# Two-layer diffusion transformer: value products of two heads side by side, scores in three passes, and bias rows and stores moved to other places

## The chip, the cores and the metric

The kernel runs on one core of one Trainium2 chip. The metric is the device time of one execution in microseconds (us), the median of several runs. The engines are TensorE (PE in the profile, its weight loads PEld), VectorE (DVE), ScalarE (ACT), GpSimd (POOL) and SyncE (SP), whose queue starts most transfers.

## The reference

Two layers work on 256 latent and 256 context tokens of width 1024. Each layer mixes tokens along three branches, gates and sums them, projects the sum, and then does a retrieval over 16384 experts by product keys. In the last layer, only the latent tokens have queries, gates and retrieval.

```
for l in range(2):
    m = silu(c) @ ada_w[l] + ada_b[l]            # 6 x 1024 modulation values, for latent and for context
    h = rmsnorm(x) * (1 + scale) + shift         # the same for ctx
    f, p, q, k, v, gates = split(h @ w_in[l])
    # 8 heads of 64, 2 key/value heads; latent queries see 512 keys, context queries 256
    ya = softmax(q @ k.T * 64 ** -0.5) @ v
    yf = fourier(f); yp = pool(p)
    x = x + m[2] * ((g0 * yf + g1 * yp + g2 * ya) @ w_out[l])
    h2 = modulate(rmsnorm(x), m[3], m[4])
    s = einsum(h2 @ wq, keys)                    # 8 heads, two halves, 128 keys each
    ...                                          # top 16 of each half, top 16 of the 256 sums
    x = x + m[5] * sum(softmax(top) * gelu(u[idx] . h2) * v[idx])
```

## The kernel before

Everything is f32 outside and runs in the order in which it is written: each engine works through its instructions in program order, and waits in front of one hold up all behind it on that engine. The helper `load` puts a transfer on SP's queue, which is in order too.

PE's large products go through `mm3`: both operands are split into a high and a low fp32r half (`split_to`: ACT writes the high half, DVE or POOL the low one), and three fp32r passes are summed. Where operands are not split, one f32 matmul stands, which the trace shows as two records: the scores (L667), the transposes of the probabilities (L685), the value products (L700), the modulation products (L333).

Weights come as items of 1 MB through a stream `S` with three raw buffers. `S.take` hands out a loaded item, `S.split` and `S.presplit` also split it, and the load of a later item waits until its buffer has been read.

**Modulation.** `ada_item(l, g, k)` adds the eighth k of group g (2048 of the 6144 values) into one PSUM bank, in four column quarters of 32 rows. At k = 0 it takes a tile `adab` for the biases, zeroes it on POOL and loads four rows with `load`. At k = 7, `finish` adds the biases on DVE. Group 0 goes into columns; groups 1 and 2 are stored to a scratch tensor `md` on SP's queue. The groups of layer 1 are computed inside layer 0: group 0 among the gate products after attention, groups 1 and 2 in the loop over heads h of the retrieval's query projection (`ada_now`).

**Attention.** Keys and queries are normalized and rotated on DVE (`rot`), transposed on PE and copied by ACT into `kT` and `qT`. Items are (pair of heads hc, block of 128 queries b, head of the pair e): 32 in layer 0, 16 in layer 1. A loop handles the scores of item n, the normalization of n - 1, the transposes of n - 2 and the value products of n - 3; steps of a gate product (`filler`, two `mm3` chains each) stand between. 24 such steps belong to the loop and 8 to the time ahead of the transposes. Both heads of a pair write into one bank `ya`, at rows 0 to 63 and 64 to 127.

**Seam after the output projection.** `wout(n, b)` makes a quarter n of the columns for block b, `wout_end(b)` stores a row block of X (`xm`) and starts its norm. `keys()` transposes the retrieval's keys, `nrm.trans(0, q)` and `nrm.cols(0, q)` the normalized latent tiles. The retrieval then projects queries for eight heads h (weights `wq`), DVE takes the top 16 of the key scores (`SC`) of each head, and the u tables follow in steps `st`, with `u_T` transposing on DVE.

Of the kernel before, what the change touches and what calls it, by code (L numbers as in the profile page):

```python
# [60 lines left out]
def kernel(ctx_: ExitStack, tc: tile.TileContext, I, C, out):  # L61
# [256 lines left out]
    md = {}  # L318
    ada_ps, ada_bt = {}, {}

    def ada_item(l, g, k):
        w = S.take(("ada", l, g, k))
        if k == 0:
            ada_ps[l, g] = psum(name="adaps")
            bt = b4([128, 2, 512], name="adab")
            ada_bt[l, g] = bt
            nc.gpsimd.memset(bt[:, 0], 0.0)
            for j in range(4):
                load(out=bt[32 * j:32 * j + 2, 0, :],
                     in_=dram(I["ada_b"], l * 6 * D + g * 2048 + j * 512, [[0, 2], [1, 512]]))  # L330
# [7 lines left out]
        def finish():  # L338
            bt = ada_bt.pop((l, g))
            nc.vector.tensor_tensor(out=bt[:, 1, :], in0=ps, in1=bt[:, 0, :], op=OP.add)  # L340
            if g == 0:
                mix_cols(l, bt[:, 1])
                return
            md[l, g] = dr_p.tile([2, 2048], F32, name=f"md{l}{g}")
            for j in range(4):
                nc.sync.dma_start(out=md[l, g][:, j * 512:(j + 1) * 512], in_=bt[32 * j:32 * j + 2, 1, :])
            if g == 2 and l == 0:
                ffn_rows(l)
# [131 lines left out]
    def mixer(l, nrm, last):  # L480
# [81 lines left out]
        kT = b4([128, 512], name="kT")  # L562
        qT = b8([128, 4, nt], name="qT")
# [79 lines left out]
        for _ in range(8):  # L643
# [4 lines left out]
        nc.scalar.activation(kT, ps, AF.Copy)  # L648
        for j in range(4):
# [3 lines left out]
            nc.scalar.activation(qT[:, j, :], ps[:, :nt], AF.Copy)  # L653
# [5 lines left out]
        def stage_scores(n):  # L659
# [7 lines left out]
            nc.tensor.matmul(ps[:, :nk], lhsT=qT[s, j, b * 128:(b + 1) * 128], rhs=kT[s, kb[0] * 128:kb[1] * 128],  # L667
                             start=True, stop=True)
# [23 lines left out]
        def stage_pv(n):  # L692
            hc, b, e = items[n]
            v = (2 * hc + e) // 4
            pT, kb = st.pop(n)
            if b == 0 and e == 0:
                ya[hc] = psum(name="ya")
            for q in range(kb[0], kb[1]):
                o = (q - kb[0]) * 128
                nc.tensor.matmul(ya[hc][64 * e:64 * e + 64, b * 128:(b + 1) * 128],  # L700
                                 lhsT=KV[:, q, 128 + 64 * v:192 + 64 * v], rhs=pT[:, o:o + 128],
                                 start=q == kb[0], stop=q == kb[1] - 1)
            if b == nq - 1 and e == 1:
# [6 lines left out]
        for n in range(N + 3):  # L710
            if 0 <= n - 1 < N:
                stage_norm(n - 1)
            if n < N:
                stage_scores(n)
# [5 lines left out]
            if n >= 3:  # L720
# [47 lines left out]
    def peer(l, nrm, kT, nb, fin):  # L768
# [263 lines left out]
        for h in range(9):  # L1032
            cur = None
            if h < 8:
                if l + 1 < DEPTH:
# [76 lines left out]
        for st in range(NSTEP):  # L1112
# [29 lines left out]
            if st == NSTEP - 10:  # L1142
                SP["keep"].discard("single")
                SP["free"] = [f for f in SP["free"] if f[1] in SP["keep"]]
                for _ in sd:
                    pass
# [223 lines left out]
```

## Time and profile before

| | us |
|---|---|
| median of 3 runs (2942.41 to 2950.72) | 2943.49 |
| profiled execution | 2943.76 |
| its span in the trace | 2942.0 |
| PE busy (94% of the span) | 2753.4 |
| DVE busy (73%) | 2158.2 |
| ACT busy (47%) | 1375.9 |
| POOL busy (44%) | 1282.2 |

The span is the time from the first to the last instruction of the profiled execution; 1.8 us lie around it. Busy time is what the engine's instructions took. PE's clock has two levels, 1.2 and 2.4 GHz; the granted clock of a stretch is the mean share of the upper one, 0.97 over the span.

### The profile page before, as it was taken

What the parts mean: (1) busy time and instruction counts of PE and PEld (TensorE: products, weight loads), DVE (VectorE), ACT (ScalarE), POOL (GpSimd) and SP (SyncE); (2) the same over time, 40 slices, a digit from 0 to 9 for tenths busy, and PEclk for the clock granted to TensorE, in tenths of its full rate; (3) what the DMA queues carried; (4) which work ended last, traced back from release to release, by engine and by line L of the source; (5) the groups of instructions that cost most, each with busy time, mean ns of one, the idle gap of its engine ahead of it and who ended that gap; (6) DMA issues with size and microseconds to landing.
All of it is one profiled execution on the core that took longest, in us unless ns stands there. A gap on an engine that the chain in (4) does not pass through costs nothing. (4 is left out here: it accounts for less than half of the span.)

```text
span 2942.0 us, 42776 instructions
## 1 busy us (share of the span) xinstructions
PE 2753.4 (94%) x16484; PEld 2403.8 (82%) x16484; DVE 2158.2 (73%) x3388; ACT 1375.9 (47%) x2243; POOL 1282.2 (44%) x698
## 2 busy tenths in 40 slices
PE   6999998799899999999999997998989989899999
PEld 4767786689888889988888886788989989888887
DVE  3444344899999985589999996555988778566666
ACT  3343223134489983333333334545446766544443
POOL 0110003237777778676666662102677655500000
PEclk8999998899999999999999999999999999899999
DMA  6215756558999999999999994337788898967775
GB/s 232 87 44 177 253 186 187 157 120 210 258 286 296 291 297 286 268 361 377 379 376 380 369 362 173 119 123 189 157 194 191 223 223 208 249 250 299 280 296 198
DMA packets 365580, 706.99 MB, mean 240 GB/s; under 512 B 25424, under 2 KB 265456, under 8 KB 351296
## 3 DMA queue, kind: packets, MB, share of 16 engines
q1 hardware_dynamic: 271104, 491.38, 56.0%
q0 software_dynamic: 36864, 134.23, 12.5%
q10 hardware_dynamic: 57408, 78.65, 7.9%
q8 instruction: 129, 2.11, 0.3%
q14 instruction: 75, 0.61, 0.1%
HBM read 619.18 MB, written 85.00 MB: 239 GB/s over the span
## 5 line engine op out<-in xcount | busy, mean ns | idle before, releaser
L1180 PE MATMUL acc<-hl,A 128*128 128x512 f32 x3840 | 871.2, 389 | 0.0
L1180 PEld LDWEIGHTS acc<-hl,A 128*128 128x128 f32 x3840 | 720.6, 188 | 150.1 <-ACT A L287 0.5
L1025 POOL TENSOR_TENSOR hl<-UT,hl 128x1024 fp32r<-128x1024 f32 x256 | 629.1, 2483 | 301.0 <-ACT hl L1018 298.9
L289 POOL TENSOR_TENSOR hl<-raw,hl 128x1024 fp32r<-128x1024 f32 x112 | 277.9, 2492 | 695.4 <-ACT hl L287 575.6
L287 ACT ACTIVATE hl<-raw 128x1024 fp32r<-128x1024 f32 x388 | 387.9, 1048 | 251.2 <-PE acc L1180 77.6
L289 DVE TENSOR_TENSOR hl<-raw,hl 128x1024 fp32r<-128x1024 f32 x276 | 349.8, 1299 | 133.5 <-ACT hl L287 133.2
L1011 DVE STREAM_TRANSPOSE UT<-raw 128x2048 f32<-128x2048 f32 x128 | 294.3, 2301 | 173.1 <-DMA raw<-in_peer_u_dram 115.0
L282 PE MATMUL ps<-hTh,hl 128*128 128x384 f32 (+2 forms) x1168 | 407.9, 349 | 4.2 <-ACT hl L1018 4.2
L284 PE MATMUL ps<-hTh,hl 128*128 128x384 f32 (+2 forms) x1168 | 402.0, 344 | 6.1 <-POOL hl L1025 6.1
L283 PE MATMUL ps<-hTl,hl 128*128 128x384 f32 (+2 forms) x1168 | 401.7, 344 | 3.5 <-POOL hTl L289 3.5
L284 PE MATMUL ps<-hT,hl 128*128 128x256 f32 x1152 | 333.7, 290 | 9.8 <-POOL hl L1025 9.8
L282 PE MATMUL ps<-hT,hl 128*128 128x256 f32 x1152 | 337.7, 293 | 1.6 <-ACT hl L1018 1.6
L283 PE MATMUL ps<-hT,hl 128*128 128x256 f32 x1152 | 333.3, 289 | 1.1 <-POOL hT L289 1.1
L1018 ACT ACTIVATE hl<-UT 128x1024 fp32r<-128x1024 f32 x256 | 256.6, 1051 | 140.1 <-DVE UT L1011 116.8
L287 ACT ACTIVATE A<-af 128x768 fp32r<-128x768 f32 (+1 forms) x128 | 94.4, 738 | 333.3 <-PE acc L1180 178.2
L282 PEld LDWEIGHTS ps<-hTh,hl 128*128 128x128 f32 x1168 | 224.8, 192 | 20.9 <-issue 4.9
L284 PEld LDWEIGHTS ps<-hT,hl 128*128 128x128 f32 x1152 | 228.4, 198 | 11.6 <-POOL hl L1025 11.6
L284 PEld LDWEIGHTS ps<-hTh,hl 128*128 128x128 f32 x1168 | 224.6, 192 | 12.1 <-POOL hl L1025 7.4
L283 PEld LDWEIGHTS ps<-hTl,hl 128*128 128x128 f32 x1168 | 225.1, 193 | 8.0 <-POOL hTl L289 3.7
L282 PEld LDWEIGHTS ps<-hT,hl 128*128 128x128 f32 x1152 | 229.6, 199 | 2.0 <-ACT hl L1018 2.0
L289 DVE TENSOR_TENSOR A<-af,A 128x768 fp32r<-128x768 f32 (+1 forms) x128 | 142.9, 1117 | 119.5 <-ACT A L287 119.5
L283 PEld LDWEIGHTS ps<-hT,hl 128*128 128x128 f32 x1152 | 229.0, 199 | 1.6 <-POOL hT L289 1.6
(245 smaller groups left out, 4795.8 us busy)
## 6 DMA issues: line engine op xcount, KB each, us to landing
raw<-in_peer_u_dram SPq DMA_DIRECT2D x512, 256.0 KB
raw<-in_peer_v_dram SPq DMA_DIRECT2D x128, 1024.0 KB
raw<-in_ada_w_dram SPq DMA_DIRECT2D x48, 1024.0 KB
G<-stg ACTq DMA_DIRECT2D x20, 2048.0 KB
raw<-in_w_in_dram SPq DMA_DIRECT2D x34, 1024.0 KB
Gq<-G SPq DMA_DIRECT2D x16, 1536.0 KB
H<-Hg ACTq DMA_DIRECT2D x56, 384.0 KB
Hq<-H SPq DMA_DIRECT2D x14, 1536.0 KB
```

The costliest lines, as they stand in the source:

```text
L282: nc.tensor.matmul(ps, lhsT=lh, rhs=rh, start=first, stop=False)
L283: nc.tensor.matmul(ps, lhsT=lh, rhs=rl, start=False, stop=False)
L284: nc.tensor.matmul(ps, lhsT=ll, rhs=rh, start=False, stop=last)
L287: nc.scalar.activation(hi, src, AF.Copy)
L289: eng.tensor_tensor(out=lo, in0=src, in1=hi.bitcast(F32), op=OP.subtract)
L1011: nc.vector.transpose(t, r)
L1018: nc.scalar.activation(t[:, 0, a], v[:, a], AF.Copy)
L1025: nc.gpsimd.tensor_tensor(out=t[:, 1, a], in0=v[:, a], in1=t[:, 0, a].bitcast(F32), op=OP.subtract)
L1180: nc.tensor.matmul(acc[b][n], lhsT=a4[:, lhs, a, t], rhs=rhs[:, o:o + 512], start=f, stop=e)
```

## The change

Six things change.

1. Keys and queries are split into halves (`kT` and `qT` become lists of two), and a score is an `mm3`. Four of the eight gate steps that stood ahead of the transposes now stand between them, one after each group of queries.
2. `stage_pv` runs every second step and handles both heads of a pair: for each block of keys, the matmul of head 0 and then that of head 1. The normalization of n - 1 now stands behind the scores of n.
3. `adab` has 512 columns instead of 2 x 512 and is taken from another pool of buffers (four of them); the sum is written over the biases.
4. The four bias rows of a group are loaded from POOL's queue.
5. The stores of layer 1's groups 1 and 2 are kept in a list and issued at h == 6 and at st == 3.
6. At the seam in layer 0, both remaining quarters of a latent block are projected together; keys and latent tiles are transposed between the quarters of the context blocks, and the columns of the latent tiles are made ahead of the last quarter.

```diff
         if k == 0:
             ada_ps[l, g] = psum(name="adaps")
-            bt = b4([128, 2, 512], name="adab")
+            bt = b1([128, 512], name="adab")
             ada_bt[l, g] = bt
-            nc.gpsimd.memset(bt[:, 0], 0.0)
+            nc.gpsimd.memset(bt, 0.0)
             for j in range(4):
-                load(out=bt[32 * j:32 * j + 2, 0, :],
+                nc.gpsimd.dma_start(
+                     out=bt[32 * j:32 * j + 2, :],
                      in_=dram(I["ada_b"], l * 6 * D + g * 2048 + j * 512, [[0, 2], [1, 512]]))
...
-            nc.vector.tensor_tensor(out=bt[:, 1, :], in0=ps, in1=bt[:, 0, :], op=OP.add)
+            nc.vector.tensor_tensor(out=bt, in0=ps, in1=bt, op=OP.add)
...
-            for j in range(4):
-                nc.sync.dma_start(out=md[l, g][:, j * 512:(j + 1) * 512], in_=bt[32 * j:32 * j + 2, 1, :])
-            if g == 2 and l == 0:
+            def store():
+                for j in range(4):
+                    nc.sync.dma_start(out=md[l, g][:, j * 512:(j + 1) * 512], in_=bt[32 * j:32 * j + 2, :])
+
+            if l:
+                stores.append(store)
+                return
+            store()
+            if g == 2:
                 ffn_rows(l)
...
         filler = fill()
-        for _ in range(8):
+        for _ in range(4):
             next(filler)
...
-        nc.scalar.activation(kT, ps, AF.Copy)
+        kT = [b4([128, 512], F32R, name="kT") for _ in range(2)]
+        qT = [b8([128, 4, nt], F32R, name="qT") for _ in range(2)]
+        split_to(kT[0], kT[1], ps)
         for j in range(4):
...
-            nc.scalar.activation(qT[:, j, :], ps[:, :nt], AF.Copy)
+            split_to(qT[0][:, j, :], qT[1][:, j, :], ps[:, :nt])
+            next(filler)
...
-            nc.tensor.matmul(ps[:, :nk], lhsT=qT[s, j, b * 128:(b + 1) * 128], rhs=kT[s, kb[0] * 128:kb[1] * 128],
-                             start=True, stop=True)
+            qh, ql = (t[s, j, b * 128:(b + 1) * 128] for t in qT)
+            kh, kl = (t[s, kb[0] * 128:kb[1] * 128] for t in kT)
+            mm3(ps[:, :nk], qh, ql, kh, kl, True, True)
...
+            two = [st.pop(n - 1), st.pop(n)]
+            kb = two[0][1]
             for q in range(kb[0], kb[1]):
                 o = (q - kb[0]) * 128
-                nc.tensor.matmul(ya[hc][64 * e:64 * e + 64, b * 128:(b + 1) * 128],
-                                 lhsT=KV[:, q, 128 + 64 * v:192 + 64 * v], rhs=pT[:, o:o + 128],
-                                 start=q == kb[0], stop=q == kb[1] - 1)
+                for e, (pT, _) in enumerate(two):
+                    nc.tensor.matmul(ya[hc][64 * e:64 * e + 64, b * 128:(b + 1) * 128],
+                                     lhsT=KV[:, q, 128 + 64 * v:192 + 64 * v], rhs=pT[:, o:o + 128],
+                                     start=q == kb[0], stop=q == kb[1] - 1)
...
         for n in range(N + 3):
+            if n < N:
+                stage_scores(n)
             if 0 <= n - 1 < N:
                 stage_norm(n - 1)
-            if n < N:
-                stage_scores(n)
...
-            if n >= 3:
+            if n >= 3 and n % 2 == 0:
                 stage_pv(n - 3)
...
             if h < 8:
+                if h == 6:
+                    for f in stores:
+                        f()
+                    stores.clear()
...
+            if st == 3:
+                for f in stores:
+                    f()
+                stores.clear()
...
             wo[2] = S.split(("wout", l, 2))
-            for b in range(nb):
-                wout(2, b)
             wo[3] = S.split(("wout", l, 3))
             kr = S.take(("keys", l)).rearrange("p (a d) -> p a d", d=128)
             for b in range(2):
+                wout(2, b)
                 wout(3, b)
-            wout_end(0)
+                wout_end(b)
+            S.presplit(True)
+            wout(2, 2)
             wout(3, 2)
-            wout_end(1)
-            S.presplit(True)
-            wout(3, 3)
             kT = keys()
+            wout(2, 3)
             for q in range(4):
                 nrm.trans(0, q)
+            for q in range(4):
+                nrm.cols(0, q)
+            wout(3, 3)
             for b in (2, 3):
                 wout_end(b)
-            for q in range(4):
-                nrm.cols(0, q)
```

How the instructions stand on the engines, at three places. A row is a line, an operation with output and inputs, a shape, and the number of like instructions in a row. First PE in layer 0's attention, at the change from latent to context items, where two steps have no gate work between them; `ps<-kT,qT` are scores, `ps<-ident,ring` transposes of probabilities, `ya<-ring,KV` value products. Before:

```order
L685 MATMUL ps<-ident,ring 128x128 x4
L700 MATMUL ya<-ring,KV 64x128 x4
L667 MATMUL ps<-kT,qT 128x256
L685 MATMUL ps<-ident,ring 128x128 x4
L700 MATMUL ya<-ring,KV 64x128 x4
L667 MATMUL ps<-kT,qT 128x256
```

Now:

```order
L282 MATMUL ps<-kT,qT 128x256
L283 MATMUL ps<-kT,qT 128x256
L284 MATMUL ps<-kT,qT 128x256
L695 MATMUL ps<-ident,ring 128x128 x4
L713 MATMUL ya<-ring,KV 64x128 x8
```

Each score has become three rows, and value products stand in groups of eight (two heads by four blocks of keys) at every second step instead of groups of four at each.

Second PE at the seam after the output projection; `ps<-hl,mg` are products of `wout`, L1229 (L1250 in the changed kernel) the transposes of `keys()`, `ps<-ident,xn` those of the latent tiles, `adaps` the first three eighths of layer 1's group 1, which `ada_now` puts ahead of head 0. Before:

```order
L284 MATMUL ps<-hl,mg 128x256
L1229 MATMUL ps<-ident,raw 128x128 x16
L451 MATMUL ps<-ident,xn 128x128 x16
L333 MATMUL adaps<-raw,cT 32x512 x12
L282 MATMUL ps<-hTh,hl 128x256
```

Now, with 24 rows of `wout` left out at either mark:

```order
L1250 MATMUL ps<-ident,raw 128x128 x16
L282 MATMUL ps<-hl,mg 128x256
...
L459 MATMUL ps<-ident,xn 128x128 x16
L282 MATMUL ps<-hl,mg 128x256
...
L335 MATMUL adaps<-raw,cT 32x512 x12
L282 MATMUL ps<-hTh,hl 128x256
```

Both groups of transposes have moved ahead of the last `wout` products.

Third SP's queue in the loop over heads; `raw` are the stream's buffers, `md` the scratch tensors of layer 1's groups 1 and 2. Before:

```order
L198 DMA raw<-in_ada_w_dram 128x2048 x3
L346 DMA md_3971<-adab 2x512 x4
L204 DMA raw<-in_peer_wq_dram 32x8x256 x4
L329 DMA adab<-in_ada_b_dram 2x512 x4
L198 DMA raw<-in_ada_w_dram 128x2048 x2
...
L204 DMA raw<-in_peer_wq_dram 32x8x256 x4
L218 DMA raw<-in_peer_u_dram 32x8x256 x4
L346 DMA md_4486<-adab 2x512 x4
L218 DMA raw<-in_peer_u_dram 32x8x256 x240
```

Now:

```order
L198 DMA raw<-in_ada_w_dram 128x2048 x3
L204 DMA raw<-in_peer_wq_dram 32x8x256 x4
L198 DMA raw<-in_ada_w_dram 128x2048 x2
...
L198 DMA raw<-in_ada_w_dram 128x2048 x2
L349 DMA md_4042<-adab 2x512 x4
L204 DMA raw<-in_peer_wq_dram 32x8x256 x4
L218 DMA raw<-in_peer_u_dram 32x8x256 x32
L349 DMA md_4557<-adab 2x512 x4
L218 DMA raw<-in_peer_u_dram 32x8x256 x212
```

The first store has moved behind all modulation loads, to the last load of wq, and the second behind 32 transfers of u; the bias loads are gone from this queue.

## Rows read from the trace of the kernel before

**Rows 1.** Windows: busy us by engine (instructions), granted PE clock, DMA share, GB/s.
```profile
526.00:541.50 15.50, 0.95 (x9) 0.20 (x8) 8.06 (x41) 3.30 (x5) 2.16 (x1) 0.59 0.64 184
...
596.00:640.00 44.00, 37.97 (x196) 35.07 (x195) 44.00 (x205) 13.92 (x20) 14.16 (x6) 0.90 0.59 129
446.00:482.00 36.00, 22.96 (x154) 17.14 (x156) 12.86 (x26) 14.32 (x27) 12.54 (x8) 0.76 0.69 204
132.90:238.70 105.80, 104.80 (x521) 68.65 (x523) 44.50 (x131) 49.16 (x117) 15.26 (x8) 1.00 0.12 41
1872.00:1934.00 62.00, 61.77 (x380) 43.84 (x378) 27.85 (x67) 32.06 (x69) 17.49 (x8) 1.00 0.22 70
```

**Rows 2.** Timeline of PE in attention, layer 0: start us, duration us.
```profile
190.45 1.12 PE L667 MATMUL ps<-kT,qT 64*128 64x512 f32 x2
191.50 0.50 PE L282 MATMUL gate<-hTh,hl 128*128 128x512 f32 x1
191.84 0.40 PE L283 MATMUL gate<-hTl,hl 128*128 128x512 f32 x1
...
192.77 0.39 PE L284 MATMUL gate<-hTh,hl 128*128 128x512 f32 x1
...
193.53 0.65 PE L700 MATMUL ya<-ring,KV 128*64 128x128 f32 x4
194.11 1.12 PE L667 MATMUL ps<-kT,qT 64*128 64x512 f32 x2
...
197.18 1.09 PE L700 MATMUL ya<-ring,KV 128*64 128x128 f32 x8
198.20 0.70 PE L667 MATMUL ps<-kT,qT 64*128 64x256 f32 x2
198.83 0.66 PE L685 MATMUL ps<-ident,ring 128*128 128x128 f32 x4
```

**Rows 3.** Timeline of PE at a modulation product.
```profile
342.73 1.92 PE L333 MATMUL adaps<-raw,cT 128*32 128x512 f32 x16
```

**Rows 4.** Groups by shape on DVE: busy us, mean ns, idle before.
```profile
L289 DVE TENSOR_TENSOR mg<-gt,mg 128x512 fp32r<-128x512 f32 x4 | 2.8, 693 | 2.9 <-ACT mg L287 2.9
```

**Rows 5.** Timeline of PE at the seam after the output projection; brackets: idle before, releaser.
```profile
442.97 1.91 PE L1229 MATMUL ps<-ident,raw 128*128 128x128 f32 x16
444.71 1.91 PE L451 MATMUL ps<-ident,xn 128*128 128x128 f32 x16
455.29 5.29 PE L333 MATMUL adaps<-raw,cT 128*32 128x512 f32 x24 [8.67 <-DVE hTf L472]
...
466.36 1.47 PE L451 MATMUL ps<-ident,xn 128*128 128x128 f32 x12
```

**Rows 6.** Timeline of SP's queue at the same seam.
```profile
445.33 0.86 SPq L1258 DMA_DIRECT2D xm<-X  x2
447.99 0.33 SPq L198 DMA_DIRECT2D raw<-in_ada_w_dram  x1
456.81 1.46 SPq L329 DMA_DIRECT2D adab<-in_ada_b_dram  x4
458.37 1.80 SPq L204 DMA_DIRECT2D raw<-in_peer_wq_dram  x4
```

**Rows 7.** Timeline of SP's queue at the two stores.
```profile
529.74 1.16 SPq L346 DMA_DIRECT2D md<-adab  x4
...
534.39 1.66 SPq L198 DMA_DIRECT2D raw<-in_ada_w_dram  x2
...
593.33 1.14 SPq L346 DMA_DIRECT2D md<-adab  x4
```

**Rows 8.** Timeline of PE behind the first store.
```profile
540.62 1.93 PE L333 MATMUL adaps<-raw,cT 128*32 128x512 f32 x8 [14.55 <-DMA raw<-in_ada_w_dram]
...
545.40 0.80 PE L282 MATMUL ps<-hTh,hl 128*128 128x512 f32 x1
```

**Rows 9.** Timeline of DVE at the same place.
```profile
541.70 0.30 DVE L791 MAX8 T1v<-SC 128x8 f32<-128x128 f32 x1 [7.63 <-ACT SC L1064]
```

More of the change, by code (lines that the diff above doesn't have):

```diff
@@ L318 @@
     md = {}
+    stores = []
     ada_ps, ada_bt = {}, {}
@@ L339, in finish @@
             bt = ada_bt.pop((l, g))
-            nc.vector.tensor_tensor(out=bt[:, 1, :], in0=ps, in1=bt[:, 0, :], op=OP.add)
+            nc.vector.tensor_tensor(out=bt, in0=ps, in1=bt, op=OP.add)
             if g == 0:
-                mix_cols(l, bt[:, 1])
+                mix_cols(l, bt)
                 return
             md[l, g] = dr_p.tile([2, 2048], F32, name=f"md{l}{g}")
-            for j in range(4):
-                nc.sync.dma_start(out=md[l, g][:, j * 512:(j + 1) * 512], in_=bt[32 * j:32 * j + 2, 1, :])
-            if g == 2 and l == 0:
+            def store():
[6 more added lines that the diff above has]
+            if g == 2:
                 ffn_rows(l)
@@ L560, in rot @@
                 nc.vector.tensor_tensor(out=src, in0=src, in1=t, op=OP.add)
-        kT = b4([128, 512], name="kT")
-        qT = b8([128, 4, nt], name="qT")
         for b in range(4):
@@ L692, in stage_pv @@
         def stage_pv(n):
[L693 to L696, printed above, removed]
+            hc, b, _ = items[n]
+            v = 2 * hc // 4
+            if b == 0:
                 ya[hc] = psum(name="ya")
+            two = [st.pop(n - 1), st.pop(n)]
+            kb = two[0][1]
             for q in range(kb[0], kb[1]):
                 o = (q - kb[0]) * 128
-                nc.tensor.matmul(ya[hc][64 * e:64 * e + 64, b * 128:(b + 1) * 128],
-                                 lhsT=KV[:, q, 128 + 64 * v:192 + 64 * v], rhs=pT[:, o:o + 128],
-                                 start=q == kb[0], stop=q == kb[1] - 1)
-            if b == nq - 1 and e == 1:
+                for e, (pT, _) in enumerate(two):
+                    nc.tensor.matmul(ya[hc][64 * e:64 * e + 64, b * 128:(b + 1) * 128],
+                                     lhsT=KV[:, q, 128 + 64 * v:192 + 64 * v], rhs=pT[:, o:o + 128],
+                                     start=q == kb[0], stop=q == kb[1] - 1)
+            if b == nq - 1:
                 split_to(yh[:, 4 + hc, :], yl[:, 4 + hc, :], ya.pop(hc)[:, :nt])
```

## The prediction, made before the change was run

> **What bounds the kernel now.** I read the span in stretches first [rows 1], because the share of busy time over the whole run mixes stages with different limits. The reader should look for stretches in which TensorE (PE) is busy without a break, since there only shorter PE work helps, and for stretches with holes, since there a wait does. The two attention stretches are of the first kind: PE is busy 104.80 of 105.80 us in layer 0 and 61.77 of 62.00 in layer 1, at granted clock 1.00, while VectorE (DVE) and ScalarE (ACT) have half their time free (44.50 and 49.16 of 105.80). The seam between output projection and retrieval (446 to 482) is of the second: PE works 22.96 of 36.00 us, at a mean clock of 0.76. So is 526 to 541.5, with 0.95 us of PE work. The row 596:640 is a third kind: DVE fills all 44.00 us and PE has holes of 6.0, so DVE is the bound there.
>
> Then I read the timeline of PE inside attention for the price of each step [rows 2], and the timelines of PE, SP and DVE across the two seams for who released whom [rows 5 to 9].
>
> **Scores in three passes.** A score item of 512 keys holds PE from 190.45 to 191.50, 1.05 us, and one of 256 keys from 198.20 to 198.83, 0.63 [rows 2]. It is an f32 matmul, which the trace shows as two records. What one record streams comes from the value products: eight records take 1.02 us (197.18 to 198.20) and four take 0.58 (193.53 to 194.11), so a record of 128 columns costs 0.11 and a group 0.14 on entry. Scaled by columns, 512 columns cost 0.44 per record and 256 cost 0.22; entry and exit of a score are then 1.05 - 0.88 = 0.17 and 0.63 - 0.44 = 0.19. The fp32r passes of the gates run 0.23 us apart at 512 columns (191.84 to 192.77, four steps [rows 2]) and 0.12 at 256 (460.58 to 466.36, 48 passes [rows 5]). New slots: 0.17 + 3 x 0.23 = 0.87, which saves 0.18, and 0.19 + 3 x 0.12 = 0.55, which saves 0.08. Layer 0 has 16 items of each kind (two latent and two context blocks by eight heads), layer 1 has 16 of 512: 16 x 0.18 + 16 x 0.08 = 4.2 us and 16 x 0.18 = 2.9 us. Bounds: 0, if the three passes pay an entry each; twice this, if the entry vanishes because the gate passes around them have the same form.
>
> **Paired value products.** Before, one head's product (64 output rows, so half the array's columns) runs alone: two items cost 2 x 1.02 or 2 x 0.58. Now both heads' products alternate between the two column halves. Do halves overlap? Before never does it in this line. The nearest row is the modulation product, which writes four column quarters with different moving data: 16 records of 512 columns take 1.92 us [rows 3], where one after the other they would take 16 x 0.44 = 7.0. So quarters do run at once, in f32, and I take halves to do so in full: a pair costs one slot, saving 1.02 or 0.58. Layer 0: 8 x 1.02 + 8 x 0.58 = 12.8 us; layer 1: 8 x 1.02 = 8.2. The lower bound is no overlap, where only one entry of 0.14 per pair goes: 2.2 and 1.1 us.
>
> The Trainium skill bears on this ("TensorE: Matmul & The Clock Gate", Part 3, Measured speedup vs the span model): it lists 2.38 times for three column tiles, less than three. An estimate from that page is 0.79 per tile, so 1.59 times for two; a 512 pair would then stream 1.11 us in place of my 0.88, and the forecast would be about 4.6 us higher. The row above has 7.0 / 1.92 = 3.6 times for four, nearer to full overlap, and I go by the row.
>
> **What attention pays.** Keys and queries now need a high and a low half: five more DVE splits per layer, 0.69 us each [rows 4], and ACT's copies stay. Four gate steps stand between them (one after each query group), which cover them on PE; I charge one uncovered split, 0.7 us, per layer. If the cover failed, all five cost 3.5 us. The transposes come four gate steps earlier, when the rotated keys must be ready; DVE's work on those lies ahead in the same queue and has half the stretch free. DVE now takes the maximum of item n ahead of the normalization of item n - 1. An item then has about 2.8 us of PE to it (90 us over 32 items), and DVE at most (44.50 + 3.5) / 32 = 1.5, so PE stays the bound. Attention in sum: 12.8 + 4.2 - 0.7 = 16.3 us in layer 0, 8.2 + 2.9 - 0.7 = 10.4 in layer 1.
>
> **The seam after the output projection.** Before, PE's last products start ahead of 442.97, the keys' and the latent tiles' transposes follow, and PE then stands 8.67 us until 455.29 [rows 5], with the modulation products waiting for PSUM banks that DVE frees late. Those products run to 460.58 at half clock (5.29 us for 24 records; the 16 of [rows 3] took 1.92). Now both groups of transposes, 1.74 us each (442.97 to 444.71), lie between wout products, so the last wout ends at 442.97 + 3.5 = 446.5 and DVE's column work is done under it: the bank wait goes. What is late next is a load. The third of the modulation loads stands on SP behind the rows of X for blocks 2 and 3, which were issued 2.36 us after PE's last wout (445.33 against 442.97 [rows 6]); so it goes out near 449.4. A load of this kind took 540.62 - 534.39 = 6.2 us from issue to its first product [rows 7, 8]; 455.6. Two of the three eighths are done by then; the last, at half clock, takes 5.29 / 3 = 1.8: 457.4 against 460.58, a gain of 3.2.
>
> Behind it, SP stood from 448.3 to 456.81, because the bias loads wait for POOL's memset, and issued wq1 only at 458.37 [rows 6]. With the bias off SP, wq1 goes out 8 us sooner, ACT and POOL split it sooner, and the later tiles' low halves on POOL are no longer behind that split. PE's two later holes there, 13.04 - 8.67 = 4.4 us in all [rows 1, 5], shrink to what the tiles themselves need, say 1.5: a gain of 2.9. The mean clock of 0.76 [rows 1] says that PE also ran at half speed behind these holes; with fewer of them I take 0.9 for it. In sum 7.0 us; bounds 0 (all of it refilled by the late load) and 12 (no load late).
>
> The Trainium skill speaks against the move to POOL's queue ("Trainium Kernel Development and Optimization", Key Constraints): DMAs of all queues share the same engines, and issuing from several saves only the issuing time. By that rule the move would be worth 1.46 us here, the four issues at 456.81, in place of 2.9, and the forecast 1.4 us higher. The row shows beside the issues 8.5 us of in-order waiting, which the move ends too.
>
> **The stores of layer 1's rows.** SP issues four stores at 529.74, when DVE has got to the sum; the modulation loads behind them go out at 534.39 [rows 7], and PE, idle since 540.62 - 14.55 = 526.07, starts at 540.62 and reaches the next projection at 545.40 [rows 8]. Placed at h == 6 and st == 3, the stores find their sums done, and this hole closes: 545.40 - 526.07 = 19.3 us, less the two modulation products at full clock, 2 x 0.96 by [rows 3], is 17.4 for PE. But the end of this stage is DVE's. DVE lost only 7.63 us to it, waiting for scores until 541.70 [rows 9], and from 596 to 640 it has no pause at all [rows 1]. Its transposes of the first u tiles stand in order behind the top-16 work, and PE's holes in that row, 6.0 us, are waits for them. So PE will run ahead and wait there for longer; the gain is DVE's 7.6 us. POOL pays for the biases: a memset and four triggers per group, at most a few us each; between seams it is idle (15.26 busy of 105.80), so nothing on the path. At the start of the program loads wait for buffers, and I count 0 (bounds 0 and 1). After 640 everything keeps its order and shifts.
>
> **Sum** against the profiled execution, 2943.76 us (span 2942.0 and 1.8 around it; the median is 2943.49, no different): 16.3 + 7.0 + 7.6 + 10.4 = 41.3, so 2902.5.
>
> **Rivals.** (a) Column halves do not overlap. For it: 64-column records of this line never did. Against: [rows 3]. Pairs then save 3.3 instead of 21.0 us: about 2920. (b) DVE is not the bound after the stores, so PE keeps its 17.4: about 2893. For it: DVE's queue has filler work that could move. Against: 44.00 of 44.00. (c) Gains are refilled: the seam after wout gives 0 because of the late load, and half of attention's gain is lost to waits for ACT's exponentials and copies: 41.3 - 7.0 - 13.4 = 20.9, about 2923. Against: ACT's 49 of 106. (d) The other side. The store at st == 3 stands on SP ahead of the remaining u loads; if DVE has not reached the second sum when SP gets there, every later u load waits, and PE with it. For it: SP did stand at this sum until 593.33 [rows 7]. Against: 32 transfers of u are now ahead of the store, where 4 were. It decides from a delay of 41 us on, which eats the sum: from 50 us on, about 2952, the change is measurably slower. (e) The change does nothing visible, because the reading of the tables, not PE or DVE, sets the end and starts when it did: about 2943. Against: the first table loads stand on SP behind wq loads, whose buffers PE frees, so their start moves with PE.
>
> **Chances.** Forecast 0.60, its own range 2893 to 2913; (a) 0.10; (b) 0.12; (c) 0.11; (e) 0.04; (d) 0.03. 0.3% of the time, 8.8 us, is about what a measurement of this kernel can tell from no change; faster by more than that holds the forecast, (a), (b) and (c), 0.93; within it (e), 0.04; slower (d), 0.03. The range 2887 to 2925 takes in the cases (a), (b) and (c) with little beyond them, and leaves out (d), (e) and what lies at the edges of the bounds.
>
> **What would show it.** In the profile after: value products of 512 keys as groups of 16 records in about 1.0 us (2.0 would show (a)); score slots of 0.87; the attention stretch about 90 us in layer 0; PE's hole after the transposes moved behind the second modulation product, released by a DMA; no md row on SP between the wq loads; no hole of 14 us near 500; DVE without a pause there, and PE waits of some 16 us in all for the first u tiles, ten more than before. The forecast is wrong if attention's clock falls below 1.00, or if those waits stay at 6.

## The result, and the profile after

The changed kernel takes 2907.62 us (median of 6 runs, 2904.93 to 2912.59), the kernel before 2943.58 (6 runs, 2939.07 to 2950.72). The ratio is 0.988, 95% interval 0.9865 to 0.9895: about 36 us faster, 5 us less than forecast. The profiled execution has a span of 2905.7 us.

The first rows answer to [rows 1]: windows of the changed kernel for the two attentions, the seam after the output projection, the heads around the old first store, and the start of the u tables. Columns: length, then busy us of PE, PEld, DVE, ACT and POOL, granted clock, DMA share, GB/s.

```profile
125.70:221.40 95.70, 95.00 (x578) 68.56 (x580) 47.80 (x137) 51.19 (x120) 27.46 (x23) 1.00 0.15 48
1849.70:1906.00 56.30, 55.91 (x428) 44.61 (x428) 31.71 (x75) 34.63 (x75) 19.34 (x8) 1.00 0.30 97
429.00:465.00 36.00, 21.13 (x143) 17.03 (x146) 9.21 (x25) 10.12 (x19) 11.43 (x10) 0.81 0.70 172
495.00:515.00 20.00, 18.06 (x105) 12.72 (x98) 20.00 (x104) 4.32 (x7) 7.29 (x7) 1.00 0.52 159
...
570.00:620.00 50.00, 35.45 (x166) 32.08 (x167) 50.00 (x222) 12.36 (x17) 14.08 (x6) 0.81 0.36 79
```

Both attentions are still PE's alone, at full clock (the windows begin four gate steps earlier than in [rows 1], because the transposes do). The seam is no better: 21.13 us of PE work in 36.00, where it was 22.96. The hole of [rows 8] is gone (18.06 of 20.00), and at the u tables PE has holes of 14.6 us in 50.00 where it had 6.0 in 44.00, while DVE is full.

Where the time went is read by leads: the start of the same instruction in the first trace of before, less its start in the other trace. Instructions are matched by order; us, so a lead that grows is time won in between.

| version | start of layer 0's mixing | end of its attention | key scores, head 0 | first u transposes (DVE) | first v products | layer 1's mixing | its keys | end |
|---|---|---|---|---|---|---|---|---|
| start in before | 105.3 | 238.6 | 493.8 | 593.2 | 1274.7 | 1856.2 | 2031.6 | 2942.0 |
| changed kernel | 1.6 | 17.3 | 16.1 | 20.4 | 18.6 | 19.0 | 30.4 | 36.3 |
| the same, second profile | 0.5 | 16.2 | 16.5 | 20.9 | 16.3 | 16.6 | 27.9 | 33.7 |
| before, second profile | 0.9 | 0.8 | 1.1 | 1.2 | 2.3 | 1.6 | 1.5 | 8.0 |
| attention part alone | 1.2 | 16.5 | 16.5 | 16.4 | 12.7 | 12.3 | 23.6 | 29.7 |
| old order at the seam | 0.2 | 15.9 | 17.4 | 21.7 | 16.2 | 15.7 | 25.5 | 31.3 |
| bias rows on SP | 0.5 | 15.8 | 19.9 | 31.0 | 27.6 | 27.3 | 38.6 | 44.2 |
| stores at once | -1.7 | 14.0 | 18.2 | 18.3 | 21.1 | 19.8 | 29.3 | 37.9 |
| X rows on ACT's queue | 0.6 | 16.3 | 24.3 | 28.6 | 26.8 | 27.4 | 38.7 | 50.6 |
| head after head in a pair | -0.2 | 12.1 | 13.7 | 18.0 | 18.6 | 18.7 | 25.6 | 28.7 |
| short pieces on POOL | -0.3 | 15.5 | 18.4 | 28.9 | 27.0 | 27.0 | 36.8 | 31.7 |
| second store on ACT | -1.7 | 14.1 | 14.6 | 18.9 | 19.2 | 19.1 | 28.9 | 35.4 |
| three edits | -0.9 | 14.8 | 18.7 | 29.3 | 34.5 | 34.7 | 44.6 | 51.0 |
| three edits, one split on DVE | -1.5 | 14.3 | 24.2 | 34.8 | 37.5 | 37.2 | 47.0 | 53.4 |

Times are medians over runs; leads are one execution each. Three steps of the table are not the change's, as far as is shown:

- The first column is a draw: versions whose start is the same code lie between -1.7 and 1.6.
- From layer 1's keys to the end, before itself gains 6.4 us (1.5 to 8.0) in its second profile, and every other version gains 3 to 12 us there as well (short pieces on POOL only from its first u transposes on). So the first trace of before was slow in that stretch.
- From layer 1's mixing to its keys, the attention itself gains 9.6 us (from the start of the mixing to the instruction behind the last value product 77.8 us in before, 68.3 in the changed kernel and in every version whose value products alternate). The rest is the clock just behind it. There PE stands 1.3 to 1.6 us for a gate product's operand, and over 15 us (the columns are those of the windows above), first in before, then in the changed kernel and last with the old order at the seam, the granted clock is 0.89, 1.00 and 0.89 (1.00 is the upper level throughout, 0.89 a mean over both levels):

```profile
1944.00:1959.00 15.00, 12.65 (x91) 12.23 (x91) 8.25 (x13) 7.92 (x12) 0.00 (x0) 0.89 0.55 179
1915.00:1930.00 15.00, 12.93 (x106) 12.52 (x105) 9.71 (x14) 7.92 (x12) 0.00 (x0) 1.00 0.58 190
1919.00:1934.00 15.00, 12.92 (x94) 12.51 (x93) 8.22 (x11) 7.93 (x12) 0.00 (x0) 0.89 0.53 174
```

Five traces have 1.00 there and gain 11.3 us up to the keys; those with alternating value products and 0.89 gain 9.5 to 9.9.

**Attention.** The timeline of PE in the changed kernel answers to [rows 2]:

```profile
183.66 0.50 PE L282 MATMUL ps<-kT,qT 64*128 64x512 f32 x1
184.00 0.39 PE L283 MATMUL ps<-kT,qT 64*128 64x512 f32 x1
184.23 0.39 PE L284 MATMUL ps<-kT,qT 64*128 64x512 f32 x1
...
187.73 1.09 PE L713 MATMUL ya<-ring,KV 128*64 128x128 f32 x16
188.75 0.38 PE L282 MATMUL ps<-kT,qT 64*128 64x256 f32 x1
```

Sixteen records, both heads, take 187.73 to 188.75: 1.02 us, the price that one head had. The three passes of a score start 0.34 and 0.23 us apart.

**The seam.** PE and then SP's queue in the changed kernel, which answer to [rows 5, 6]:

```profile
431.53 1.92 PE L335 MATMUL adaps<-raw,cT 128*32 128x512 f32 x16 [2.20 <-ACT junk L442]
443.37 1.93 PE L335 MATMUL adaps<-raw,cT 128*32 128x512 f32 x8 [9.92 <-DMA raw<-in_ada_w_dram]
...
457.52 0.39 PE L283 MATMUL ps<-hTl,hl 128*128 128x256 f32 x1 [2.44 <-POOL hTl L289]
```

```profile
423.73 0.33 SPq L198 DMA_DIRECT2D raw<-in_ada_w_dram  x1
424.11 8.13 SPq L1279 DMA_DIRECT2D xm<-X  x2
432.28 0.43 SPq L198 DMA_DIRECT2D raw<-in_ada_w_dram  x1
432.81 3.36 SPq L204 DMA_DIRECT2D raw<-in_peer_wq_dram  x4
```

The wait for banks is gone and a wait for the third load has come: issued at 432.28 behind the rows of X, used at 443.37, 11.1 us later where 6.2 were assumed. The wq load goes out only 0.5 us behind it. The record of packets shows where the time went (packets by size between 434.3 and 438, then between 438 and 442.5; the load has 128 packets, all of 8 KB, and the wq load's have 1 KB):

```profile
DMA packets 268, 1.03 MB, mean 277 GB/s; under 512 B 60, under 2 KB 153, under 8 KB 155
DMA packets 719, 0.78 MB, mean 173 GB/s; under 512 B 65, under 2 KB 702, under 8 KB 704
```

113 of the load's packets start within 5.7 us of its issue, and the last 15 trickle out among the wq load's until 442.4. In the row of before that gave the 6.2 us, the wq load had been issued ahead of the modulation load:

```profile
531.00 1.81 SPq L204 DMA_DIRECT2D raw<-in_peer_wq_dram  x4
```

There all 128 packets start within 5.3 us of the issue.

**The top-16 stretch.** DVE and POOL in the changed kernel:

```profile
503.97 0.74 DVE L825 TENSOR_TENSOR cand<-T1v 128x256 f32<-128x256 f32 x2
...
523.56 4.69 DVE L825 TENSOR_TENSOR cand<-T1v 128x256 f32<-128x256 f32 x2
```

```profile
523.08 4.89 POOL L289 TENSOR_TENSOR hl<-raw,hl 128x1024 fp32r<-128x1024 f32 x2 [8.43 <-ACT hl L287]
```

Two such additions of candidate lists take 0.74 us alone, and 4.69 when POOL's two wq splits run beside them. Which heads meet a split depends on when POOL's splits come, and so on the loads and PE's heads.

### The profile page after: what moved, and what is told of

It is laid out like the page before. It is cut to its first block, busy times and chain, and to the rows that moved or that the text cites. A ratio compares the mean times of both kernels' runs of the same rounds, so it can differ in the third digit from the quotient of the medians.

```text
span 2905.7 us, 42921 instructions
## 1 busy us (share of the span) xinstructions
PE 2721.5 (94%) x16532; PEld 2394.1 (82%) x16532; DVE 2164.8 (74%) x3398; ACT 1374.7 (47%) x2243; POOL 1290.3 (44%) x722
## 5 line engine op out<-in xcount | busy, mean ns | idle before, releaser
L284 PEld LDWEIGHTS ps<-hT,hl 128*128 128x128 f32 x1152 | 227.4, 197 | 11.3 <-POOL hl L1038 11.3
```

Of the source, the lines that this page charges most:

```text
L284: nc.tensor.matmul(ps, lhsT=ll, rhs=rh, start=False, stop=last)
```

## The experiments

Each edit is on the changed kernel, except where it says otherwise. A ratio is to the kernel before, measured beside the run. The changed kernel itself has 0.988 (0.9865 to 0.9895) and, in experiment 10, 0.9882 (0.9867 to 0.9897); a version whose interval overlaps these is not shown to be faster or slower than the changed kernel.

**1. X rows on ACT's queue.**

```diff
-            nc.sync.dma_start(out=xm[b], in_=X[:, b, :])
+            (nc.scalar if b >= 2 else nc.sync).dma_start(out=xm[b], in_=X[:, b, :])
```

> The changed kernel, but the rows of X for blocks 2 and 3 are stored from ACT's queue instead of SP's, so the third modulation load at the seam no longer stands behind them. Theory A (the hole of 9.9 us at the seam is that load, issued late behind those stores at 432.3 and then sharing the transfer engines with the four wq loads): it goes out near 424, lands near 431, PE's hole shrinks to under 3 us, the work after it starts 7 to 9 us earlier, and the run is 6 to 9 us faster than the changed kernel, about 2900. Rival B (the three loads in a row are limited by the rate of the transfers, whatever the order): the hole keeps 6 us or more, and the run stays within 3 us of 2907.

Measured 2896.63 us, ratio to before 0.9832 (0.9805 to 0.9858). PE and SP:

```profile
432.52 4.44 PE L335 MATMUL adaps<-raw,cT 128*32 128x512 f32 x24 [2.20 <-ACT junk L442]
```

```profile
424.71 0.81 SPq L198 DMA_DIRECT2D raw<-in_ada_w_dram  x2
434.50 1.92 SPq L204 DMA_DIRECT2D raw<-in_peer_wq_dram  x4
```

Theory A: both loads go out at 424.71, all three eighths run in one piece, and the seam gains 8.0 us (16.3 to 24.3) where the changed kernel loses 1.2. The interval lies wholly below the changed kernel's. The other half of theory A, that the load also suffers from sharing with the wq load, is not separated from it by this edit.

**2. Old order at the seam** (the last hunk of the diff undone).

> The changed kernel with the order of before at the seam after the output projection (the projections of both remaining quarters, then transposes, then columns); everything else of the change stays. Theory A (the new order only swaps a wait for PSUM banks for a wait for the load, and nothing is won): the lead over the kernel before at the second head's key scores is 14 to 18 us, where the changed kernel has 16.1, and the run is within 3 us of 2907. Rival B, that of the prediction (the order is worth about 4 of its 7 us and something else ate them): the lead there is 10 to 13 us and the run 3 to 6 us slower than the changed kernel.

Measured 2911.66, ratio 0.9879 (0.9852 to 0.9905). PE, and then what SP's queue waited for between 428 and 445 (us in total, times, longest):

```profile
439.05 4.50 PE L335 MATMUL adaps<-raw,cT 128*32 128x512 f32 x24 [8.30 <-DVE hTf L480]
```

```profile
SPq L204 <- PE adaps L335: 8.5, 1, 8.5
```

PE's hole of 8.30 before the modulation products is back, as before. The seam gains 1.5 us and the ratio is the changed kernel's; the median is 4 us longer, which is rival B's figure, but before's beside it is 4 us longer too (2947.45). Theory A: the new order swapped one wait for another.

The second line answers a step of the prediction. In before, SP stood at the bias rows for POOL's memset:

```profile
SPq L329 <- POOL adab L327: 8.5, 1, 8.5
```

Here no bias rows are on SP, and the wq load stands just as long, because its buffer is free only when PE has read the modulation item in it. So in the old order the move of the bias rows did not end that wait; the seam gains 1.5 us with them off SP (this run) and 0.0 with them on it (experiment 9).

**3. Bias rows on SP.**

```diff
-                nc.gpsimd.dma_start(
+                load(
```

> The changed kernel with the bias rows loaded from SP's queue again, at the places where the kernel before has them. Theory A (off SP they save only 1.6 us at the start of the program; at the seam the hold on SP kept the wq loads from sharing the transfer engines with the modulation load, so its end costs what it brings): the lead in front of layer 0's attention falls from 1.6 to 0, the modulation load at the seam takes 8 to 11 us, the run is 1 to 3 us slower than the changed kernel, 2908 to 2911. Rival B, that of the prediction (the move is worth 2.9 us at the seam as well): 4 to 6 us slower. Rival C (the small transfers from POOL slow the large load beside them): the seam is 3 us shorter than in the changed kernel and the run 1 to 2 us faster.

Measured 2899.68, ratio 0.9842 (0.9815 to 0.9869): rival C's sign, but more than it says and not its cause. The seam gains 4.1 us, with a hole of 6.58; but stores at once, with the seam of the changed kernel unchanged, also gains 4.2 there, so that can be a draw of the load's time and need not be the queue's doing. The large part comes behind it: 11.1 us on DVE (19.9 to 31.0), where the changed kernel gains 4.3. The groups of the additions say why (xcount, then busy us and mean ns), for the 18 ahead of the first u transposes, here:

```profile
L825 DVE TENSOR_TENSOR cand<-T1v 128x256 f32<-128x256 f32 x18 | 9.3, 553 | 0.0
```

and in the changed kernel:

```profile
L825 DVE TENSOR_TENSOR cand<-T1v 128x256 f32<-128x256 f32 x18 | 17.0, 986 | 0.0
```

7.7 us less, because fewer meet POOL. This is no draw of one execution: the six traces with the bias rows on POOL's queue, both stores late and POOL's pieces long all gain 4.3 or 4.4 us in this stretch. SP, here first and then in the changed kernel, shows what shifts the phase:

```profile
503.82 1.14 SPq L330 DMA_DIRECT2D adab<-in_ada_b_dram  x4
505.06 0.83 SPq L198 DMA_DIRECT2D raw<-in_ada_w_dram  x2
```

```profile
497.97 0.87 SPq L198 DMA_DIRECT2D raw<-in_ada_w_dram  x2
```

The bias rows hold the next modulation loads on SP, and POOL's splits behind them lie otherwise against DVE's additions. Nothing in the change aims at that, and that this shift makes the difference is argued from one trace. But as it stands, point 4 of the change may cost more than it brings: the intervals of the two versions barely touch.

**4. Stores at once.**

```diff
-            if l:
-                stores.append(store)
-                return
             store()
-            if g == 2:
+            if g == 2 and l == 0:
```

> The changed kernel, but layer 1's modulation rows are stored at once, as before, so SP stands at the first store until DVE has the sum. Theory A (DVE's top-16 work is the bound from about 480 to 660, and PE's hole of 14 to 17 us only takes the place of later waits): PE's hole near 510 comes back, DVE stands 6 to 8 us, and the run is 0 to 5 us slower than the changed kernel, since the second store no longer holds the table loads at 640. Rival B (PE's hole counts in full): 13 to 17 us slower, about 2922.

Measured 2901.82, ratio 0.9851 (0.9811 to 0.989), its runs from 2896.80 to 2914.18. PE and DVE:

```profile
522.44 1.93 PE L335 MATMUL adaps<-raw,cT 128*32 128x512 f32 x8 [14.54 <-DMA raw<-in_ada_w_dram]
```

```profile
523.57 0.29 DVE L801 MAX8 T1v<-SC 128x8 f32<-128x128 f32 x1 [7.68 <-ACT SC L1078]
```

PE's hole and DVE's are back in full, and the run is no slower. Rival (b) of the prediction, that PE's hole counts, is out. The later stores win 4.3 us at the first u transposes (0.1 here), and the lead at the first v products is no larger for it (2.5 us from the scores on, against 3.0 here).

**5. Head after head in a pair.** The loop over heads stands outside that over key blocks.

```diff
-            for q in range(kb[0], kb[1]):
-                o = (q - kb[0]) * 128
-                for e, (pT, _) in enumerate(two):
+            for e, (pT, _) in enumerate(two):
+                for q in range(kb[0], kb[1]):
+                    o = (q - kb[0]) * 128
```

> The changed kernel, but within a pair all value products of head 0 stand ahead of those of head 1, so the two column halves no longer alternate; the pairing into one group stays. Theory A (the gain of pairing is that alternating halves run at once; the merged entry is worth 0.14 us a pair): a pair of 512 keys takes 1.8 to 2.0 us instead of 1.02, the lead at the end of layer 0's attention falls from 15.7 to 4 to 6 us and layer 1's from 11 to 3 to 5, and the run is 15 to 19 us slower than the changed kernel. Rival B (halves overlap whatever the order, since PE looks ahead): a pair takes 1.0 to 1.2 us and the run stays within 3 us.

Measured 2914.64, ratio 0.9893 (0.9864 to 0.9921).

```profile
175.01 1.58 PE L713 MATMUL ya<-ring,KV 128*64 128x128 f32 x16
180.15 0.66 PE L713 MATMUL ya<-ring,KV 128*64 128x128 f32 x8
```

Between the two theories: a pair of 512 keys (eight records of one half, then eight of the other) takes 1.58 us by the row instead of 1.09, a pair of 256 keys (four and four) loses nothing. Attention's lead falls from 15.7 to 12.4 us in layer 0 and from 9.6 to 6.7 in layer 1 (both to the end of the attention), so alternating is worth 6.2 us in all; what is left of the gain does not need it. Theory A's 15 to 19 us more are out; the interval overlaps the changed kernel's.

**6. Short pieces on POOL.**

```diff
-                    split_to(t[:, 0, w], t[:, 1, w], r[:, w], pool or (self.half and h == 1))
+                    if key[0] == "wq":
+                        nc.scalar.activation(t[:, 0, w], r[:, w], AF.Copy)
+                        for i in range(h * 4, h * 4 + 4):
+                            x = slice(i * 256, i * 256 + 256)
+                            nc.gpsimd.tensor_tensor(out=t[:, 1, x], in0=r[:, x], in1=t[:, 0, x].bitcast(F32), op=OP.subtract)
+                    else:
+                        split_to(t[:, 0, w], t[:, 1, w], r[:, w], pool or (self.half and h == 1))
```

> The changed kernel, but POOL makes the low halves of each wq item in eight pieces of 256 columns instead of two of 1024. Theory A (DVE's sums of two candidate lists, 0.40 us alone, take up to 2.6 us when they meet one of POOL's splits, because they wait for its end; 17.7 us go into 18 of them ahead of the first u transposes): with short pieces none takes over 1.2 us, the 18 take 8 to 11 us together, DVE reaches the first u transpose 6 to 9 us sooner after its first top-16 work, and the run is 4 to 9 us faster than the changed kernel. Rival B (the sums are slow for another reason, or wait for POOL's whole row of pieces): they take 16 to 19 us as now, and the run is within 3 us.

Measured 2913.90, ratio 0.9897 (0.9869 to 0.9924): not faster, though theory A holds in layer 0, but for one addition of 2.2 us. The 18 additions there take

```profile
L831 DVE TENSOR_TENSOR cand<-T1v 128x256 f32<-128x256 f32 x18 | 10.8, 640 | 0.0
```

and the top-16 stretch gains 10.5 us (18.4 to 28.9) instead of 4.3. In layer 1 the run loses 15.7 between its keys and its first u transposes (lead 36.8 to 21.1), and the 16 additions there take 40.8 us against 22.7, summed over their records. One of them is the whole difference. DVE and POOL:

```profile
2023.59 23.93 DVE L831 TENSOR_TENSOR cand<-T1v 128x256 f32<-128x256 f32 x1
```

```profile
2008.25 38.98 POOL L164 TENSOR_TENSOR hl<-raw,hl 128x256 fp32r<-128x256 f32 x56 [0.79 <-ACT hl L161]
```

The 56 pieces run to 2047.23 without a pause, and the addition that starts among them ends at 2047.52, just behind the last. So here rival B holds: the addition waits for POOL's whole row. In layer 0 a row has eight pieces and then a pause of some 8 us. With long splits in the changed kernel, the first addition at 523.56 ends 0.3 us behind the first of the two; what decides whether a piece lets an addition in is open.

**7. Second store on ACT's queue** (the store at st == 3 issued with `nc.scalar.dma_start`).

> The changed kernel, but the second store of layer 1's rows, at st == 3, is issued from ACT's queue instead of SP's. Theory A (on SP it stands in front of the table loads from 640 to 648, and DVE stands 6.25 us for one of them at 655): DVE does not stand there, the lead of its u transposes stays at 20 us through the ninth instead of falling to 14, and the run is 0 to 5 us faster than the changed kernel, since later waits have taken part of it back already. Rival B (the loads wait for buffers and for H's stores, not for this store): the lead falls to 14 to 16 all the same, and the run is within 2 us.

Measured 2901.20, ratio 0.9849 (0.9822 to 0.9877). DVE first in the changed kernel, then here:

```profile
661.23 2.31 DVE L1024 STREAM_TRANSPOSE UT<-raw 128x2048 f32<-128x2048 f32 x1 [6.25 <-DMA raw<-in_peer_u_dram]
```

```profile
644.28 2.31 DVE L1024 STREAM_TRANSPOSE UT<-raw 128x2048 f32<-128x2048 f32 x1 [1.40 <-DMA raw<-in_peer_u_dram]
```

The lead at the ninth u transpose falls by 1.5 us (18.9 to 17.4) instead of 6.5 (20.4 to 13.9). The other versions agree: with the second store late on SP's queue it falls by 6.1 to 7.0 us there (six more traces), with it at once or on ACT's queue by 0.1 to 0.6 (stores at once and the two versions with three edits). Theory A for the place. What it is worth at the end is not shown: from the scores to the first v products this version gains 4.6 us, the changed kernel 2.5 in its first profile and -0.2 in its second, and the intervals overlap.

**8. Before, a second profile.**

> The kernel before, unchanged, for a second profile: the changed kernel gains 6 us in layer 1's retrieval, of which the change touches nothing that I can name. Theory A (executions of one kernel differ there by several us): this profile differs from the first one between layer 1's keys and its last stage by 3 us or more. Theory B (the change does shorten it, by other buffers): it agrees within 2 us, and all versions of the changed kernel stay 5 us or more below.

One execution, 2935.8 us. It ends 8.0 us ahead of the first profile, 6.4 of that behind layer 1's keys. Theory A: the 5.9 us that the changed kernel shows there prove nothing about the change. Nor are they refuted, since the first profile's time is at the median of before's runs and this one's is among the shortest.

**9. The attention part alone**, on the kernel before: the hunks of attention, with the smaller bias tile (still loaded by SP), old seam, stores at once.

> The kernel before with the attention part of the change alone (three-pass scores, paired value products, their order, the smaller bias tile); the seam, the bias loads and the stores stand as before. Theory A (attention's gain passes through the retrieval whole): the lead at the end of layer 0's attention is 15 to 16 us and 13 to 17 at the end of layer 0, layer 1's attention adds 10 to 11.5, and the run is 24 to 29 us faster than the kernel before. Rival B (the retrieval's loads and DVE take part of it back, and the rest of the change was what brought the lead): under 18 us faster.

Measured 2913.14 against 2946.09 for before beside it, ratio 0.9889 (0.9874 to 0.9904). The leads are 15.3 us in layer 0's attention and 9.6 in layer 1's, 24.9 in all. Of 16.5 us behind layer 0's attention 12.3 are left at the end of layer 0, a little below what theory A says, and 3.7 are lost between the first u transposes and the first v products. By the time it is 33 us faster (28 to 37 by the interval), by the median above both theories. The 3 to 12 us beyond its attention have no cause in the edit that is shown; the table has gains behind layer 1's attention, by the clock (1.7) and in the stretch where the first trace of before was slow (6.1). Whether before's executions are slow there as a rule, two traces of it can't say.

**10. The changed kernel again**, beside experiment 9.

> The changed kernel, unchanged, beside the two others on the same chip. If the hole of 9.9 us at the seam is a draw (the same code had one of 4.8 in the version with the stores at once), it is 4 to 10 us here; attention's lead is 15.7 again; the median is 2900 to 2910.

Measured 2910.95, ratio 0.9882 (0.9867 to 0.9897); hole at the seam 8.37. Against experiment 9 on the same chip the rest of the change is worth 2 us, and the two intervals overlap almost wholly: it is not shown to be worth anything.

**11. Three edits together** (1, 6 in layer 0 only, 7).

> The changed kernel with three edits together: the rows of X for blocks 2 and 3 and the second store of layer 1's rows go out from ACT's queue, and POOL makes the low halves of wq in pieces of 256 columns, in layer 0 only. If the three waits that they remove are separate (8 us at the seam, 6 to 8 us of DVE meeting POOL's splits, about 2 us behind the second store), layer 0 ends 33 to 37 us ahead of the kernel before, layer 1's retrieval starts as in the changed kernel, and the run takes 2885 to 2895 us. Rival: they hide one another, since DVE's stretch is followed by the same table loads; then it is no faster than with the first edit alone, 2893 to 2899.

Measured 2890.37 (5 runs), ratio 0.9808 (0.9795 to 0.9822). Neither theory in full: the time is that of the first, but the seam gains only 3.8 us where edit 1 alone gained 8.0; experiment 12 tests whether POOL's pieces hold the tiles' low halves there. The interval lies below the changed kernel's, but overlaps that of edit 1 alone, whose lead at the end, 50.6 us, is no smaller than the 51.0 here.

**12. The same, with the second wq item's low half on DVE.**

```diff
-                    if key[:2] == ("wq", 0):
+                    if key[:2] == ("wq", 0) and key[2] != 1:
...
-                        split_to(t[:, 0, w], t[:, 1, w], r[:, w], pool or (self.half and h == 1))
+                        split_to(t[:, 0, w], t[:, 1, w], r[:, w], (pool or (self.half and h == 1)) and key != ("wq", 0, 1))
```

> The version with the three edits, and the low half of the second wq item made by DVE instead of POOL, so the low halves of the later tiles no longer stand behind it on POOL. Theory A (the holes of 4.3 and 4.1 us that are left at the seam come from that queue: POOL splits wq from 446.4 to 452.4 and only then the tiles): they shrink to 4 us together or less, the lead at the second head's scores grows from 4 to 7 to 9 us over the seam, and the run is 1 to 5 us faster than the one before it, 2885 to 2889. Rival B (the wq load itself, landing at 445, holds ACT and all behind it): the holes stay at 7 us or more and the time at 2890.

Measured 2889.20 (5 runs), ratio 0.9813 (0.9799 to 0.9827). PE:

```profile
447.29 0.66 PE L465 MATMUL ps<-ident,xn 128*128 128x128 f32 x4 [1.15 <-ACT hTf L488]
449.30 0.39 PE L289 MATMUL ps<-hTl,hl 128*128 128x256 f32 x1 [0.96 <-POOL hTl L295]
452.32 0.38 PE L289 MATMUL ps<-hTl,hl 128*128 128x256 f32 x1 [0.96 <-POOL hTl L295]
```

The holes shrink to 3.1 us and the seam gains 9.9: theory A for the place. In the whole run the 1.2 us to experiment 11 are inside the intervals.

## Why the prediction was right, step by step

- **Attention, 26.7 us: right, in mechanism and nearly in size.** It gave 15.7 us in layer 0 (forecast 16.3) and 9.6 in layer 1 (10.4), 25.3 in all. The pair of 512 keys cost 1.02, as forecast; a score 0.89 (183.66 to 184.55, the next row's start) against 0.87. Rival (a) is out: 16 records in the time of eight, and experiment 5 shows the overlap by taking part of it away. That the attention alone makes the kernel faster is shown by experiment 9. The Trainium skill's ratio ("TensorE: Matmul & The Clock Gate", Part 3) would, by the prediction's estimate, have put 4.6 us less here; two halves overlapped in full in this case.
- **The seam, 7.0 us: wrong.** It gave -1.2 and 0.3 in the two profiles. Two steps failed. The first is "a load of this kind took 6.2 us". In that row the wq load went ahead; here it goes out behind, and the load took 7 to 11 us from issue to use in versions with the same code at the seam. The spread is in its last packets: the last of 128 starts 9.6 us after the issue in the first profile, 5.8 with the stores at once. They run among the wq load's packets, but whether that load causes the delay was not tested by itself, and why they are late in some executions only is open. Experiment 1 shows that the hole hangs on where the load stands in SP's queue, which the prediction had named as what is late next and priced too low. The second is that SP stood "because the bias loads wait for POOL's memset", so that the move ends the wait: experiment 2 has the wq load stand 8.5 us without them, for its buffer. In the changed kernel it does go out early, because the new order lets PE read that buffer early, and PE stands for the modulation load all the same.
- **The stores, 7.6 us: the wait was rightly found, the gain was not there at the end.** PE's hole gave way to later waits, and DVE decides (experiment 4), so rival (b) is out. DVE's pauses over 0.3 us, between its first top-16 work and the first u transpose, fell from 8.2 to 0.6 us in all, but its 18 additions there went from 13.3 us (the same group in before) to 17.0, a loss of 3.7 that the prediction did not see. That left 4.3 us at the first u transposes. Then the second store, named only under rival (d), held the table loads (experiment 7): not the disaster of (d), but by the ninth u transpose the 4.3 were gone. At the first v products 2.5 us were left in one profile and -0.2 in the other, against 3.0 with the stores at once.
- **Nothing after 640: not borne out in the profile, and not refuted.** The first profile gains 5.9 us behind layer 1's keys and 1.8 by the clock behind its attention; neither can be put down to the change.

That the total came within 5 us of the forecast is in part luck. The seam and the stores brought 13 to 15 us less than forecast, and the first trace shows 9 us in places that the forecast put at nothing (1.6 at the start, 1.8 and 5.9 in layer 1). Attention's 25 us are what the change is shown to bring; the other points together are worth 2 us by experiments 9 and 10, which the intervals do not tell from none.

## What to carry to other kernels

Where an engine is busy without a break, price its instructions and the gain comes out at the end; where it has holes, ask of each removed wait which transfer, and where in its queue, is next. An order that keeps PE fed is of no use while the load that it needs stands behind a store on the same queue. DVE and POOL do not run side by side for every pair of instructions (0.74 against 4.69 us for two additions), so a shift in time alone can move several us. And a forecast that comes out in sum is checked term by term, against more than one trace of the kernel before.

## What was not expected of the hardware

An addition of two SBUF operands on DVE takes 0.40 us and up to 2.6 beside a POOL split of 2.4, and short POOL pieces brought it down in layer 0. The Trainium skill says this ("SBUF — State Buffer", SBUF: two separate sides): such a DVE instruction and a POOL instruction exclude each other for a whole instruction. The trace agrees with long splits and in most of layer 0. In layer 1 of experiment 6 it shows more: one addition waited 23.9 us, through a row of pieces of 0.7 us each, to the end of the row.

Groups of four f32 records on one column half and four on the other overlap as well as alternating ones (0.66 us), groups of eight do not (1.58 against 1.09).
